# Output projection, second half: a third pair of K tiles by seven products

## The chip, the cores and the metric

One core of a Trainium2 chip runs the whole kernel in one launch. The metric is the device time in microseconds; lower is better. Engines are named as in the profile: PE (matrix products; PEld its weight loads), DVE and ACT (elementwise work), POOL, and SP, whose queue issues most DMA loads.

## The reference, cut to what matters

Two layers, 256 tokens, model width 2048. The part in question is the output projection of the mixer:

```
mix = concat([stick-breaking heads (8 x 128), differential heads (8 x 128)])   # (256, 2048)
m   = mix @ w_o                                                                # (256, 2048)
x   = x + rms_norm(m, post_mix_norm)
h   = rms_norm(x, pre_ffn_norm)
x   = x + rms_norm((silu(h @ w_gate) * (h @ w_up)) @ w_down, post_ffn_norm)
```

Everything is float32 in and out.

## The kernel before

**Tiles.** The 256 tokens are two token tiles of 128 (t = 0, 1). A weight matrix is cut into column blocks of 512 (c) and into pairs of K tiles of 128 (kp). One load of 512 KB brings a weight tile of one pair and one column block. Float32 products are made of three matmuls: each operand is split into a rounded part (`hi`, written by ACT) and the rest (`lo`, written by DVE), and PE does hi x hi, hi x lo, lo x hi. `feed` (L297) does this split for each weight in the order of the stream: ACT at L307, DVE at L317. `raw`, `hi` and `lo` are rings in `wpool` with 4, 6 and 6 places; a new tile waits until the readers of the tile six (four) places back are done.

**Eight and seven products.** Two K tiles, two token tiles and two column blocks make a 2 x 2 by 2 x 2 block product: eight products, 24 matmuls. For some pairs the kernel uses a form with seven products (Winograd's), 21 matmuls, in `seven_products`. It needs sums of the activations (`token_sums`, called by `pair_forms`: tiles f, s, sh, sl) and sums of the weights (`mixed_weights`, L263): from the two loaded tiles g and u ACT and DVE form in turn `hi`/`lo` of g, u + g (L285), `hi`/`lo` of that (L279, L281), differences (L290, L291), and the splits `T2h`/`T2l` and `Th`/`Tl`. Four extra PSUM banks (p1, p6, p7, q5) collect products over all seven-product pairs of a stage; `shared_part` (L1125 to L1129) folds them into `mg` after the last such pair, and L1179 adds a part of `mg` to the still open sums of token tile 1.

**Output projection.** Its first half does column blocks 0 and 1 over all eight pairs while the last attention heads are still being finished. The second half does blocks 2 and 3. `LATE_O` gives the order of pairs there, `LAST_O` the two pairs that come at the very end, done token tile by token tile so that the norm of tile 0 can begin while PE works on tile 1; `O_SEVEN` names the pairs with seven products. In this kernel the order is 4, 5, 0, 1, 6, 2 and then 3, 7, with seven products for 5 and 6. Their token sums are computed in the first half, after units 9 and 11 (L1157), in places of the ring `tok`; their weights are loaded into places of the attention's ring `v` (two), and `T2h`/`T2l` lie in `ah` and `al` (one each).

**The end of the stage.** From `feed(idx + 6)` on the order of ACT and DVE is the program's (`manual_schedule`). `evac_sum` takes the sums of token tile 0 out (L589 adds `mg`, L591 squares, L592 multiplies by the gain), `rescale` forms the norm and writes `x` (L627), PE transposes it (L485), ACT and DVE split it into `xF` (L488, L493), and the gate and up products of the next stage (L1250) start. Elsewhere a scheduler orders each engine's instructions by its own costs; each engine then runs its queue in that order.

Of the kernel before, what the change touches and what calls it, by code (L numbers as in the profile page):

```python
# [9 lines left out]
F32 = mybir.dt.float32  # L10
F32R = mybir.dt.float32r
# [6 lines left out]
P = 128  # L18
D = 2048
S = 256  # L20
# [5 lines left out]
CW = 512  # L26
# [5 lines left out]
URGENT = 50  # L32
TAIL = 3
KP_O = (4, 5, 6, 7, 0, 1, 2, 3)
LATE_O = (4, 5, 0, 1, 6, 2)
LAST_O = (3, 7)
O_SEVEN = (5, 6)
PAIRS = ((6, 8), (10, 7), (9, 0), (11, 2), (1, 3), (4, 5))
IN_SEVEN = (4, 5)
IN_ORDER = (0, 1, 4, 2, 5, 3, 6, 7)  # L40
# [40 lines left out]
def weight_order():  # L81
# [9 lines left out]
    for l in range(L):  # L91
# [7 lines left out]
        order_o = [(c, kp) for kp in KP_O for c in (0, 1)]  # L99
        order_o += [(c, kp) for kp in LATE_O for c in (2, 3)] + [(c, kp) for c in (2, 3) for kp in LAST_O]  # L100
        lay["order_o"] = order_o
# [66 lines left out]
def kernel(  # L168
# [35 lines left out]
    order, plan, sevens, plain, own = weight_order()  # L204
# [3 lines left out]
    for lay in plan:  # L208
        for c in range(1, FF // CW):
            for n in (1, 2):  # L210
                helped[lay["gate"][c, gate_order(c)[n]]] = n == 1
    newest_seven = [None]

    ready = {}
    raws, loads = [], []
# [2 lines left out]
    def fetch(upto):  # L218
        while len(raws) < min(upto, len(stream)):
            i = len(raws)  # L220
            for j in range(i, min(i + EARLY + 1, mix_raw[3])):
                if j in sevens and j not in sums:
                    summed(j)
            if i in sevens:
                raws.append(sums[i])
                continue
            if i + 1 in sevens:
                g = mix_raw[0].tile([P, 2, CW], F32, tag="G", bufs=mix_raw[1], name=f"G{i}")
                with not_ahead(i):
                    loads.append(nc.sync.dma_start(g, stream[i]))  # L230
                raws.append(g)
                continue
            if i in own or i + 1 in own:
                raw = mix_pool[0].tile([P, 2, CW], F32, tag="v", bufs=2, name=f"V{i}")
            elif i in plain or i + 1 in plain:
                raw = late_room([P, 2, CW], f"GU{i}")
            else:
                raw = wpool.tile([P, 2, CW], F32, tag="raw", bufs=4, name=f"raw{i}")
            mixing = bool({i, i + 1} & (own | plain))
            with not_ahead(i) if mixing else nullcontext():  # L240
                loads.append(nc.sync.dma_start(raw, stream[i]))
            raws.append(raw)
            if not mixing:
                usual.append((i, loads[-1]))
# [15 lines left out]
    mix_pool = [None]  # L260
    mix_raw = [None, 0, 0, 0]

    def mixed_weights(i):  # L263

        g, u = raws[i - 1], raws[i]
        hi = wpool.tile([P, 2, CW], F32R, tag="hi", bufs=6, name=f"hi{i}")
        lo = wpool.tile([P, 2, CW], F32R, tag="lo", bufs=6, name=f"lo{i}")
        if i in own:
            th = wpool.tile([P, 2, CW], F32R, tag="hi", bufs=6, name=f"Th{i}")
            tl = wpool.tile([P, 2, CW], F32R, tag="lo", bufs=6, name=f"Tl{i}")  # L270
            th2 = mix_pool[0].tile([P, 2 * (S + P)], F32R, tag="ah", bufs=1, name=f"T2h{i}")[:, 0:CW]
            tl2 = mix_pool[0].tile([P, 2 * (S + P)], F32R, tag="al", bufs=1, name=f"T2l{i}")[:, 0:CW]
        else:
            th = mix_pool[0].tile([P, 3, CW], F32R, tag="Th", bufs=1 if i in plain else 2, name=f"Th{i}")
            tl = mix_pool[0].tile([P, 3, CW], F32R, tag="Tl", bufs=1 if i in plain else 2, name=f"Tl{i}")
            th2, tl2 = th[:, 2, :], tl[:, 2, :]

        def split(h, l, w):
            nc.scalar.activation(h, w, AF.Copy)  # L279
            with in_row(i):  # L280
                newest_rest[i] = nc.vector.tensor_tensor(out=l, in0=w, in1=h.bitcast(F32), op=ALU.subtract)  # L281

        if i in plain or i in own:
            with after_rests():
                nc.vector.tensor_tensor(out=u[:, 0, :], in0=g[:, 0, :], in1=u[:, 0, :], op=ALU.add)  # L285
        split(hi, lo, u)
        t1, b22 = ((hi[:, k, :], lo[:, k, :]) for k in range(2))
        t3, t4 = ((th[:, k, :], tl[:, k, :]) for k in range(2))
        t2 = u[:, 1, :]
        nc.vector.tensor_tensor(out=t2, in0=t2, in1=u[:, 0, :], op=ALU.subtract)  # L290
        nc.vector.tensor_tensor(out=g, in0=g, in1=t2.unsqueeze(1).to_broadcast([P, 2, CW]), op=ALU.add)  # L291
        split(th2, tl2, t2)
        split(th[:, 0:2, :], tl[:, 0:2, :], g)
        t2 = th2, tl2
        return {"b22": b22, "t1": t1, "t2": t2, "t3": t3, "t4": t4}
# [645 lines left out]
    def pair_forms(pool, spool, bufs, tiles, kp, nm, **kw):  # L941
        f = pool.tile([P, 2, S], F32, tag="t2", name=f"f{nm}_{kp}")
        for kk in range(2):
            st = tiles[2 * kp + kk]
            nc.vector.tensor_tensor(out=f[:, kk, :], in0=st[:, 0, :].bitcast(F32), in1=st[:, 1, :].bitcast(F32), op=ALU.add)
        return token_sums(pool, spool, bufs, f[:, 0, 0:P], f[:, 1, 0:P], f[:, 0, P:S], f[:, 1, P:S], f"{nm}_{kp}", **kw)
# [138 lines left out]
        nc.tensor.matmul(a, sh, lo, start=False, stop=False, skip_group_check=open_sums[0])  # L1085
        return nc.tensor.matmul(a, sl, hi, start=False, stop=last, skip_group_check=open_sums[0])  # L1086

    def token_sums(pool, spool, bufs, a11, a12, a21, a22, nm, tags=("sh", "sl")):

        s = pool.tile([P, 4, P], F32, tag="t2", name=f"s{nm}")  # L1090
        nc.vector.tensor_tensor(out=s[:, 0, :], in0=a21, in1=a22, op=ALU.add)
        nc.vector.tensor_tensor(out=s[:, 1, :], in0=s[:, 0, :], in1=a11, op=ALU.subtract)
        nc.vector.tensor_tensor(out=s[:, 2, :], in0=a11, in1=a21, op=ALU.subtract)
        nc.vector.tensor_tensor(out=s[:, 3, :], in0=a12, in1=s[:, 1, :], op=ALU.subtract)
        if spool is None:
            both = late_room([P, 2, 4, P], f"ss{nm}", F32R)
            sh, sl = both[:, 0], both[:, 1]
        else:
            sh = spool.tile([P, 4, P], F32R, tag=tags[0], bufs=bufs, name=f"sh{nm}")
            sl = spool.tile([P, 4, P], F32R, tag=tags[1], bufs=bufs, name=f"sl{nm}")  # L1100
        nc.scalar.activation(sh, s, AF.Copy)
        nc.vector.tensor_tensor(out=sl, in0=s, in1=sh.bitcast(F32), op=ALU.subtract)
        return [(sh[:, j, :], sl[:, j, :]) for j in range(4)]
# [31 lines left out]
    for l in range(L):  # L1135

        pool = Rooms(tc, f"att{l}")
# [5 lines left out]
        mix, mixed = {}, set()  # L1143
# [6 lines left out]
        forms = {}  # L1150
        for n, (c, kp) in enumerate(plan[l]["order_o"][:16]):
            run_until(lambda: mixed >= {2 * kp, 2 * kp + 1})
            unit({t: accs[c, t] for t in range(NT)}, mix, plan[l]["o"][c, kp], kp, range(NT), kp == KP_O[0], kp == KP_O[-1])
            if kp == KP_O[-1]:
                for t in range(NT):
                    evac_chunk(pool, accs[c, t], mg, ssm, gpost, c, t, f"o{l}")
            if n in (9, 11):  # L1157
                kp = O_SEVEN[(n - 9) // 2]
                forms[kp] = pair_forms(pool, pool, 4, mix, kp, f"o{l}", tags=("tok", "tok"))
        got = four_banks(True, [f"o{l}_{c}_{t}" for t in range(NT) for c in (2, 3)])  # L1160
        accs = {(c, t): got[2 * t + c - 2] for c in (2, 3) for t in range(NT)}
        open_sums[0] = True
        for kp in LATE_O:
            i, j = (plan[l]["o"][c, kp] for c in (2, 3))
            if kp not in O_SEVEN:
                for c, i in ((2, i), (3, j)):
                    unit({t: accs[c, t] for t in range(NT)}, mix, i, kp, range(NT), kp == LATE_O[0], False)
                continue
# [12 lines left out]
        xT = x_tiles(f"xF{l}")  # L1181
        idx = plan[l]["o"][2, LAST_O[0]]
        last_o = [(c, kp) for c in (2, 3) for kp in LAST_O]
        with tc.manual_schedule(engines={mybir.EngineType.Activation, mybir.EngineType.DVE}):
            feed(idx + 6)
            for n, (c, kp) in enumerate(last_o):
                unit({0: accs[c, 0]}, mix, idx + n, kp, (0,), False, kp == LAST_O[-1], 0)
                if kp == LAST_O[-1]:
                    evac_sum(pool, accs[c, 0], mg, ssm, gpost, c, 0, f"o{l}")
# [16 lines left out]
        pool = tc.alloc_tile_pool(name=f"ffn{l}", bufs=5, reuse_waits="tile")  # L1206
        gu = tc.alloc_tile_pool(name=f"gu{l}", bufs=1, reuse_waits="tile")
# [5 lines left out]
        forms = {}  # L1213
# [45 lines left out]
        for c in range(FF // CW):  # L1259
# [9 lines left out]
            for n, kp in enumerate(order):  # L1269
# [13 lines left out]
                if kp == mine[-1]:  # L1283
                    w = [pool.tile([P, CW], F32, tag="t2", name=f"w{j}_{l}_{c}") for j in range(4)]
# [38 lines left out]
        for half in range(2):  # L1323
            split, forms = {}, {}
# [73 lines left out]
            for t in range(NT):  # L1398
# [4 lines left out]
                for c in cc:  # L1403
                    for kp in range(nkp - tail, nkp):
# [4 lines left out]
                        for kk in range(2):  # L1409
                            sh, sl = jh[:, kk, t * P : (t + 1) * P], jl[:, kk, t * P : (t + 1) * P]  # L1410
# [64 lines left out]
```

## Time and profile before

| | |
|---|---|
| time, median of 3 runs | 2182.53 us (2181.71 to 2182.81) |
| profiled execution, device time | 2183.48 us |
| its span, first to last instruction | 2181.7 us |
| busy PE / DVE / ACT / POOL | 2166.0 / 1920.7 / 1400.4 / 260.5 us |
| second half of the output projection, first layer | about 350.8 to 393 us |
| the same, second layer | about 1436.8 to 1479 us |
| granted clock of TensorE | 0.999 |

Times in the profile count from the first instruction of the span. A row of a timeline gives start, duration, engine, line, operation, output and inputs, count, and in brackets how long the engine was idle before it and what it waited for. A row of the chain gives start, length, engine and line. A row of the groups ends with the busy time of all, the mean in ns of one, and the idle time before them. A row of the waits gives the total, the number and the longest. A row of a windows view gives the length, then busy time and number of instructions of PE, PEld, DVE, ACT and POOL, the clock, the DMA share and GB/s. A matmul's duration overlaps the next one's, so its cost is read from the starts. All lines are those of the kernel before.

### The profile page before, as it was taken

The numbers are of one execution on the slowest core, as the hardware profiler recorded it, in microseconds if no ns is written. First come the engines' busy times: TensorE is split into PE (matmuls) and PEld (weight loads), VectorE is DVE, ScalarE is ACT, GpSimd is POOL, SyncE is SP. The second block draws the span as 40 slices with busy tenths as digits, with TensorE's granted clock in tenths as the row PEclk, the third lists the DMA queues.
The fourth block names the chain that finished last, engine by engine and source line by source line (L and its number), as shares of the span: only waits on it lengthen the run. The fifth ranks groups of instructions, "written<-read, shape, count | busy, mean of one in ns | idle before, by whom it ended". The sixth has DMA issues, their size and how long they took to land.

```text
span 2181.7 us, 28784 instructions
## 1 busy us (share of the span) xinstructions
PE 2166.0 (99%) x9944; PEld 1781.7 (82%) x9944; DVE 1920.7 (88%) x2657; ACT 1400.4 (64%) x2089; POOL 260.5 (12%) x243
## 2 busy tenths in 40 slices
PE   9999999999999999999999999999999999999998
PEld 7888888788888888888878888887888888888886
DVE  7888658899999999999878886589999999999997
ACT  7666665756666656666665666657666666576664
POOL 1100000031222221000010000000212222200000
PEclk9999999999999999999999999999999999999999
DMA  9544555488887767767465555555888877768683
GB/s 323 194 164 174 193 184 176 165 300 234 239 258 229 226 231 233 239 223 258 149 241 174 172 174 188 191 164 191 286 237 241 262 222 227 240 225 244 204 268 100
DMA packets 140851, 471.49 MB, mean 216 GB/s; under 512 B 16016, under 2 KB 17040, under 8 KB 140192
## 3 DMA queue, kind: packets, MB, share of 16 engines
q1 hardware_dynamic: 121952, 436.03, 57.7%
q0 software_dynamic: 18176, 33.07, 9.2%
q8 instruction: 78, 1.28, 0.2%
q14 instruction: 69, 0.57, 0.1%
q10 hardware_dynamic: 576, 0.54, 0.1%
HBM read 461.19 MB, written 8.39 MB: 215 GB/s over the span
## 4 chain that ended last, share of the span: by engine, by line
PE 94%; DVE 3%; ACT 2%; issue 1%; DMA 0%; SPq 0%; DVEq 0%; ACTq 0%
PE c L1250 19%; PE in L1084 7%; PE in L1086 7%; PE in L1085 7%; PE dn L1357 4%; PE dn L1356 4%; PE dn L1359 4%; PE p L1085 3%; PE c L1084 3%; PE p L1084 3%; PE p L1086 3%; PE c L1085 3%; PE c L1086 3%; PE o L569 2%; PE o L571 2%; PE o L570 2%
## 5 line engine op out<-in xcount | busy, mean ns | idle before, releaser
L317 DVE TENSOR_TENSOR lo<-raw,hi 128x1024 fp32r<-128x1024 f32 x468 | 561.9, 1220 | 103.3 <-ACT hi L307 102.3
L307 ACT ACTIVATE hi<-raw 128x1024 fp32r<-128x1024 f32 x490 | 501.5, 1053 | 102.3 <-DMA raw<-in_weights_in_turn_dram 41.8
L1250 PE MATMUL c<-hi,xF 128*128 128x512 f32 x1280 | 345.9, 391 | 1.5 <-DVE xF L493 1.5
L1250 PEld LDWEIGHTS c<-hi,xF 128*128 128x128 f32 x1280 | 238.3, 188 | 50.3 <-DVE xF L493 2.0
L258 POOL DMA_DIRECT2D T<-in_weights_in_turn_dram x126 | 111.2, 883 | 1373.8 <-DMA T<-in_weights_in_turn_dram 716.6
L1250 PE MATMUL c<-lo,xF 128*128 128x512 f32 x640 | 198.2, 390 | 2.5 <-DVE lo L317 2.5
L279 ACT ACTIVATE Th<-G 128x1024 fp32r<-128x1024 f32 x126 | 133.1, 1056 | 79.8 <-DVE G L291 78.6
L281 DVE TENSOR_TENSOR Tl<-G,Th 128x1024 fp32r<-128x1024 f32 x126 | 153.9, 1221 | 10.1 <-ACT Th L279 10.1
L1356 PE MATMUL dn<-hi,jh 128*128 128x512 f32 x416 | 162.0, 389 | 0.0
L1357 PE MATMUL dn<-lo,jh 128*128 128x512 f32 x416 | 161.8, 389 | 0.0
L307 ACT ACTIVATE hi<-G 128x1024 fp32r<-128x1024 f32 x126 | 132.9, 1055 | 44.6 <-DMA G<-in_weights_in_turn_dram 27.8
L281 DVE TENSOR_TENSOR lo<-T,hi 128x1024 fp32r<-128x1024 f32 x126 | 159.6, 1266 | 0.3 <-ACT hi L279 0.2
L279 ACT ACTIVATE Th<-T 128x512 fp32r<-128x512 f32 x126 | 79.7, 633 | 118.6 <-DVE T L290 113.3
L291 DVE TENSOR_TENSOR G<-G,T 128x1024 f32<-128x1024 f32 x126 | 153.5, 1218 | 1.8
L1250 PEld LDWEIGHTS c<-lo,xF 128*128 128x128 f32 x640 | 120.1, 188 | 28.1 <-DVE lo L317 3.0
L317 DVE TENSOR_TENSOR lo<-G,hi 128x1024 fp32r<-128x1024 f32 x108 | 131.6, 1219 | 12.3 <-ACT hi L307 12.2
L279 ACT ACTIVATE hi<-T 128x1024 fp32r<-128x1024 f32 x126 | 132.2, 1049 | 12.1 <-PE c L1086 10.6
L1084 PE MATMUL in<-hi,xT 128*128 128x512 f32 x328 | 131.0, 401 | 0.6 <-DVE xT L862 0.6
L1084 PE MATMUL in<-hi,xI 128*128 128x512 f32 x328 | 131.1, 401 | 0.0
L1085 PE MATMUL in<-lo,xI 128*128 128x512 f32 x328 | 128.0, 390 | 0.3 <-DVE lo L317 0.3
L1085 PE MATMUL in<-lo,xT 128*128 128x512 f32 x328 | 127.8, 391 | 0.4 <-DVE lo L891 0.4
L1359 PE MATMUL dn<-hi,jl 128*128 128x512 f32 x416 | 128.0, 389 | 0.0
(485 smaller groups left out, 4954.2 us busy)
## 6 DMA issues: line engine op xcount, KB each, us to landing
raw<-in_weights_in_turn_dram SPq DMA_DIRECT2D x490, 512.0 KB, 4.6
T<-in_weights_in_turn_dram SPq DMA_DIRECT2D x126, 512.0 KB, 5.3
G<-in_weights_in_turn_dram SPq DMA_DIRECT2D x126, 512.0 KB, 5.4
T<-in_weights_in_turn_dram POOLq DMA_DIRECT2D x126, 256.0 KB, 6.1
GU<-in_weights_in_turn_dram SPq DMA_DIRECT2D x32, 512.0 KB, 6.5
V<-in_weights_in_turn_dram SPq DMA_DIRECT2D x8, 512.0 KB, 3.7
away_ffn<-x SPq DMA_DIRECT2D x8, 512.0 KB, 8.2
xd<-away_ffn SPq DMA_DIRECT2D x8, 512.0 KB, 9.4
```

The costliest lines, as they stand in the source:

```text
L279: nc.scalar.activation(h, w, AF.Copy)
L281: newest_rest[i] = nc.vector.tensor_tensor(out=l, in0=w, in1=h.bitcast(F32), op=ALU.subtract)
L291: nc.vector.tensor_tensor(out=g, in0=g, in1=t2.unsqueeze(1).to_broadcast([P, 2, CW]), op=ALU.add)
L307: nc.scalar.activation(hi, raw, AF.Copy)
L317: rest = nc.vector.tensor_tensor(out=lo, in0=raw, in1=hi.bitcast(F32), op=ALU.subtract)
L1084: nc.tensor.matmul(a, sh, hi, start=first, stop=False, skip_group_check=open_sums[0])
L1085: nc.tensor.matmul(a, sh, lo, start=False, stop=False, skip_group_check=open_sums[0])
L1086: return nc.tensor.matmul(a, sl, hi, start=False, stop=last, skip_group_check=open_sums[0])
L1250: nc.tensor.matmul(a, stat[part], w[j][:, kk, :], start=first and kk + n == 0, stop=last and kk == 1 and n == 2)
L1356: nc.tensor.matmul(accs[c, t], sh, hi[:, kk, :], start=first, stop=False, skip_group_check=open_sums[0])
L1357: nc.tensor.matmul(accs[c, t], sh, lo[:, kk, :], start=False, stop=False, skip_group_check=open_sums[0])
L1359: nc.tensor.matmul(accs[c, t], sl, hi[:, kk, :], start=False, stop=last, skip_group_check=open_sums[0])
```

## The change

The second half's pairs now come in the order 4, 5, 1, 7, 6, 2 and then 0, 3, and pair 7 too is done with seven products, at the fourth place. Its token sums are formed after unit 11, those of pairs 5 and 6 two units earlier than before. The added pair's tiles take places of other rings: the sums sh and sl in the ring `a`, the two loaded weight tiles in `qk` (so they no longer take places of `raw`), `T2` in `w`; `Th` and `Tl` take places of `hi` and `lo`, as for the other two.

```diff
-LATE_O = (4, 5, 0, 1, 6, 2)
-LAST_O = (3, 7)
-O_SEVEN = (5, 6)
+LATE_O = (4, 5, 1, 7, 6, 2)
+LAST_O = (0, 3)
+O_SEVEN = (5, 7, 6)
+O_FORM_AT = {7: 5, 9: 6, 11: 7}
...
+    between = {lay["o"][3, O_SEVEN[1]] for lay in plan}
+    set_aside = []
...
-            if i in own or i + 1 in own:
+            if i in between or i + 1 in between:
+                raw = set_aside.pop(0)
+            elif i in own or i + 1 in own:
                 raw = mix_pool[0].tile([P, 2, CW], F32, tag="v", bufs=2, name=f"V{i}")
...
-            th2 = mix_pool[0].tile([P, 2 * (S + P)], F32R, tag="ah", bufs=1, name=f"T2h{i}")[:, 0:CW]
-            tl2 = mix_pool[0].tile([P, 2 * (S + P)], F32R, tag="al", bufs=1, name=f"T2l{i}")[:, 0:CW]
+            th2, tl2 = (
+                mix_pool[0].tile([P, 2 * (S + P)], F32R, tag="w" if i in between else t, bufs=3 if i in between else 1, name=f"T2{t}{i}")[:, 0:CW]
+                for t in ("ah", "al")
+            )
...
-            if n in (9, 11):
-                kp = O_SEVEN[(n - 9) // 2]
-                forms[kp] = pair_forms(pool, pool, 4, mix, kp, f"o{l}", tags=("tok", "tok"))
+            if n in O_FORM_AT:
+                kp = O_FORM_AT[n]
+                if kp == O_SEVEN[1]:
+                    forms[kp] = pair_forms(pool, pool, 2, mix, kp, f"o{l}", tags=("a", "a"), width=2 * (S + P))
+                else:
+                    forms[kp] = pair_forms(pool, pool, 4, mix, kp, f"o{l}", tags=("tok", "tok"))
+            if n == 11:
+                set_aside[:] = [pool.tile([P, 2, CW], F32, tag="qk", bufs=4, name=f"V{q}_o{l}") for q in "gu"]
```

`token_sums` gets a `width` for places that are wider than the sums; nothing else changes in it.

More of the change, by code (lines that the diff above doesn't have):

```diff
@@ L1086, in product, with token_sums @@
         return nc.tensor.matmul(a, sl, hi, start=False, stop=last, skip_group_check=open_sums[0])
-    def token_sums(pool, spool, bufs, a11, a12, a21, a22, nm, tags=("sh", "sl")):
+    def token_sums(pool, spool, bufs, a11, a12, a21, a22, nm, tags=("sh", "sl"), width=4 * P):
         s = pool.tile([P, 4, P], F32, tag="t2", name=f"s{nm}")
@@ L1098, in token_sums @@
         else:
-            sh = spool.tile([P, 4, P], F32R, tag=tags[0], bufs=bufs, name=f"sh{nm}")
-            sl = spool.tile([P, 4, P], F32R, tag=tags[1], bufs=bufs, name=f"sl{nm}")
+            sh, sl = (
+                spool.tile([P, width], F32R, tag=tag, bufs=bufs, name=f"{q}{nm}")[:, 0 : 4 * P].rearrange("p (j n) -> p j n", j=4)
+                for q, tag in zip(("sh", "sl"), tags)
+            )
         nc.scalar.activation(sh, s, AF.Copy)
```

## The prediction

> **What bounds the kernel now.** I read the page first, then TensorE's waits over the whole span, then the chain that ended last, then the timelines of PE and DVE through the output projection of the first layer.
>
> ```profile
> span 2181.7 us, 28784 instructions
> ...
> PE 2166.0 (99%) x9944; PEld 1781.7 (82%) x9944; DVE 1920.7 (88%) x2657; ACT 1400.4 (64%) x2089; POOL 260.5 (12%) x243
> ```
>
> PE is without work for 2181.7 - 2166.0 = 15.7 us. So a product taken out of PE's queue is worth its time only where nothing else is late next. Where PE waits:
>
> ```profile
> PE c L1250 <- DVE lo L317: 2.5, 2, 1.3
> ...
> PE c L1250 <- DVE xF L493: 1.5, 2, 0.7
> ```
>
> Both waits are two of a kind, one in each layer, and both sit at the seam behind the output projection, where the gate products (`c`, L1250) start. The chain shows what stands ahead of them:
>
> ```profile
> 384.38 1.07 ACT hi L307
> 385.48 1.23 DVE lo L317
> ...
> 392.23 0.76 DVE x L627
> ...
> 406.21 3.70 PE c L1250 x15
> ...
> 1470.35 1.07 ACT hi L307
> ...
> 1492.17 3.75 PE c L1250 x15
> ```
>
> From 384.38 to 406.21 the end of the kernel hangs on ACT and DVE: two gate weights are split, the first token tile's sums are taken out (L589), the norm is formed, `x` is written (L627), transposed, split into `xF`. The second layer repeats it: 1470.35 to 1492.17 is 21.82 us, 384.38 to 406.21 is 21.83 us. Whatever this chain's start loses, the kernel loses, twice; PE's products beside it are cover.
>
> **What is removed: three matmuls a layer.** A pair of eight products issues 24 matmuls, one of seven 21; the order of instructions of the changed program has six rows fewer on PE. What is one worth?
>
> ```profile
> L569 PE MATMUL o<-hi,mix_sb 128*128 128x512 f32 x128 | 50.2, 392 | 0.0
> ...
> L569 PEld LDWEIGHTS o<-hi,mix_sb 128*128 128x128 f32 x128 | 24.0, 188 | 5.0
> ```
>
> ```profile
> 361.00 0.39 PE L569 MATMUL o<-hi,mix_sb 128*128 128x512 f32 x1
> ...
> 376.64 0.39 PE L569 MATMUL o<-hi,mix_sb 128*128 128x512 f32 x1
> ...
> 381.41 0.40 PE L569 MATMUL o<-hi,mix_sb 128*128 128x512 f32 x1
> ...
> 384.18 0.39 PE L569 MATMUL o<-hi,mix_df 128*128 128x512 f32 x1
> ...
> 393.04 1.32 PE L485 MATMUL xT_ps<-ident,x 128*128 128x128 f32 x8
> ...
> 396.42 1.19 PE L1250 MATMUL c<-hi,xF 128*128 128x512 f32 x4 [0.74 <-DVE xF L493]
> ```
>
> Not 392 ns: from 361.00 to 376.64 pairs 0, 1 and 6 start 24 + 24 + 21 = 69 matmuls, 15.64 / 69 = 0.227 us from start to start. So 3 x 0.227 = 0.68 us a layer, 1.36 us in all, and by itself it ends at 2182.53 - 1.36 = 2181.2. The Trainium skill (Perfetto Trace Analysis, Identifying the Most-Contended Engine) calls matmul busy time a bad measure because matmuls are pipelined, and takes the LDWEIGHTS busy time in its place: by the 188 ns of the second row six matmuls would be 1.13 us. I keep the spacing.
>
> **What is added on DVE and ACT.** The next rows are DVE's timeline.
>
> ```profile
> 332.38 0.75 DVE L945 TENSOR_TENSOR fo<-mix_df 128x256 f32<-128x256 f32 x2
> 333.05 0.28 DVE L1093 TENSOR_TENSOR so<-fo 128x128 f32<-128x128 f32 x1
> ...
> 336.46 0.68 DVE L1102 TENSOR_TENSOR slo<-so,sho 128x512 fp32r<-128x512 f32 x1
> ...
> 357.58 2.59 DVE L317 TENSOR_TENSOR lo<-raw,hi 128x1024 fp32r<-128x1024 f32 x2 [1.07 <-ACT hi L307]
> 360.31 1.23 DVE L317 TENSOR_TENSOR lo<-V,hi 128x1024 fp32r<-128x1024 f32 x1
> ...
> 363.40 1.22 DVE L281 TENSOR_TENSOR lo<-V,hi 128x1024 fp32r<-128x1024 f32 x1 [1.26 <-ACT hi L279]
> ...
> 367.81 1.23 DVE L281 TENSOR_TENSOR Tl<-V,Th 128x1024 fp32r<-128x1024 f32 x1 [0.61 <-ACT Th L279]
> 368.96 1.22 DVE L317 TENSOR_TENSOR lo<-raw,hi 128x1024 fp32r<-128x1024 f32 x1
> ...
> 375.80 0.68 DVE L1126 TENSOR_TENSOR mg_o<-p_o,mg_o 128x512 f32<-128x512 f32 x1
> ...
> 379.27 0.68 DVE L1128 TENSOR_TENSOR mg_o<-q_o,mg_o 128x512 f32<-128x512 f32 x1
> 379.87 0.68 DVE L1129 TENSOR_TENSOR mg_o<-q_o,mg_o 128x512 f32<-128x512 f32 x1
> ...
> 384.10 1.23 DVE L317 TENSOR_TENSOR lo<-raw,hi 128x1024 fp32r<-128x1024 f32 x1 [2.35 <-ACT hi L307]
> 385.48 1.23 DVE L317 TENSOR_TENSOR lo<-raw,hi 128x1024 fp32r<-128x1024 f32 x1 [0.16 <-ACT hi L307]
> 386.62 0.68 DVE L589 TENSOR_TENSOR mg_o<-o,mg_o 128x512 f32<-128x512 f32 x1
> ```
>
> The token sums of the added pair (two additions of 0.75 together, four of 0.28, one split of 0.68: 2.6 us of DVE) are computed in the first half. That stretch has room:
>
> ```profile
> 318.00:351.00 33.00, 33.00 (x160) 27.57 (x159) 24.44 (x44) 18.57 (x38) 0.00 (x0) 1.00 0.46 158
> ```
>
> DVE is free for 33.00 - 24.44 = 8.6 us there, PE never waits, so I cost the sums at nothing; without that cover they would cost at most their 2.6 us.
>
> The weight chain of a seven pair is another matter. Pair 6 holds DVE from 360.31 to 368.96, 8.65 us, ACT's answers included, while its 21 matmuls take 4.76 us. In the changed order of DVE pair 1's two splits move to the place of pair 0's, so pair 7's chain starts at 357.58, on the same freed `hi` place, and pair 6's behind it:
>
> 357.58 + 8.65 + 8.65 = 374.88. At this point DVE was at 368.96 before, 5.9 us earlier, though PE now needs the tiles 0.68 us sooner.
>
> Behind that the changed order has, one after another: four splits (pair 2, then pairs 0 and 3 for column block 2), L1126, L1127, the split of pair 0 for block 3, L1128, L1129, the first of the two L1179. Splits follow at 1.14 (385.48 to 386.62), additions at 0.60 (379.27 to 379.87), a dependent one at its 0.68 and 0.03. So 374.88 + 4 x 1.14 + 0.71 + 0.60 + 1.14 + 2 x 0.60 + 0.68 = 383.77 us for the end of that L1179. PE's second token tile may add to its open sums only after it.
>
> **What moves on PE.** Pair 2's products for the second token tile wait for L1179 in both kernels, but the changed order puts them later. Before, 21 matmuls lie between the start of pair 2 and them (376.64 to 381.41); after, 31: pair 2's first tile (12), pair 0 (6), pair 3 (6), pair 0 of block 3 (6), one of pair 3. PE alone would be there at 376.64 - 0.68 + 31 x 0.227 = 383.0; with L1179 it is 383.8. Twelve matmuls end at 386.5, where they ended at 384.18 before: 2.35 us later.
>
> **Who waits for that.** Two `hi` places become free with these products. ACT's gate splits wait for them (384.38 in the chain), DVE's `lo` behind ACT (384.10 with 2.35 us idle, 385.48), and L589, whose bank is long full, stands behind both `lo` in DVE's queue: 386.62. That is the head of the chain above. All 21.8 us of it follow 2.35 us later; PE runs out of projection at about 393 as before and stands until `x` arrives, which it used to get just in time (393.04). The 0.74 us wait before 396.42 grows by it.
>
> Sum: +2.35 us a layer, with the 0.68 us already in it; +4.7 in two. The profiled execution (2183.48 us, 1.8 us of it outside the span) lies 0.95 above the median, and both shift alike: 2182.53 + 4.7 = 2187.2 us.
>
> **The unknown term: a load.** Pair 7 leaves the `raw` ring of four, so the weight of pair 0 for block 3 gets the place of pair 2's first, free at 374.88 + 1.23 = 376.1 (before: 370.2, after the split of 368.96). How long does such a load take?
>
> ```profile
> DMA to landing us min/median/max: 3.3/4.3/5.0
> ```
>
> That is the raw loads issued from 366 to 380. I take 3.3, the row's least, since nothing else is being fetched then; it lands at 379.4, ACT's 1.06 us end before DVE comes to it (380.75). At 5.0 DVE stands 1.4 us at this split and the layer loses 3.75. At the other end, if DVE keeps up everywhere, PE's order alone costs (31 - 21 - 3) x 0.227 = 1.6 a layer. So +3.2 to +7.5 us, 2185.7 to 2190.0. Below that only if the chain has slack which I do not see: the first L627 of 392.23 is 0.76 long, the transposes start at 393.04.
>
> The other edits I cost at nothing. The two `qk` places of the added weights were last read for the scores; their loads stand in SP's queue right behind pair 2's, ahead of pair 6's. `w` and `a` places are past their last attention reader. The gate stage's first `G` load now waits for DVE, behind whose later work the raw loads of its queue wait anyway.
>
> **Rivals.**
> 1. *The gain arrives* (other side): -1.36 us, 2181.2. It needs DVE's lag gone before PE reaches pair 2's second tile: from 383.77 back to 380.7 at least, and the `hi` places free in time. For it: PE is busy for 99% of the span. Against: PE's order is fixed, and 31 matmuls stand where 21 stood. 0.05. The Trainium skill (Perfetto Trace Analysis, Identifying Performance Opportunities) says to work on the most contended engine first; by that rule this rival would be the outcome.
> 2. *The seam absorbs it*: the waits of 0.74 and 1.25 us behind the projection (2.5 + 1.5 in two layers by the waits' rows) shrink as the chain slips. Then 2.35 - 1.99 = 0.4 a layer, 2183.3. It decides if what is late there is not a successor of L589. Against: 392.23 to 406.21 is one unbroken chain. 0.08.
> 3. *The late load holds DVE*: 3.75 a layer, 2190.0. It decides above a landing of 3.5 us. For it: the median of 4.3; against: the empty queue. 0.17.
>
> My case, around 2.35 a layer, gets 0.70.
>
> **How the numbers follow.** 0.2% (4.4 us) is about what a measurement of this kernel can tell from no change, and my forecast of 4.7 lies just above. From my case I give 0.42 to slower and 0.28 to within; rival 3 is slower; rivals 1 and 2 are within it, save 0.02 for a gain I have no mechanism for. Faster 0.02, same 0.39, slower 0.59. The range, 2184.5 to 2189.8, leaves out rivals 1 and 2 and the far end of rival 3 (0.07): 0.20.
>
> **What would show it.** In the changed profile's DVE timeline L589 should stand about 2.35 us later than 386.62, with a wait of PE for DVE at pair 2's second tile, and PE's wait for DVE's `xF` at the first `c` should be near 3 us instead of 0.74. Pair 6's last `lo` (`Tl`) should end near 375, at most 0.2 us after PE asks. If L589 comes at 386 or earlier, my DVE sum is wrong; if it is late and `c` still starts at 396.4, the chain has slack that I did not see; if the `lo` of pair 0 for block 3 waits for ACT's `hi` for over a microsecond, rival 3 is at work.

## The result, and the profile after

The changed kernel takes 2190.08 us (median of 5 runs, 2187.72 to 2192.13) against 2182.53 (2181.51 to 2183.36): 1.0035 times, 95% interval 1.0024 to 1.0047, or +7.55 us. Forecast was 2187.2 us, at most 2189.8: the sign was right, the size too small. Line numbers moved: L1179 is now L1193, L589 L596, L592 L599, L627 L634, L485 L492, L1250 L1264, L317 L324, L281 L288, L230 L233, L257 and L258 L262 and L263.

DVE's timeline in the second half of the projection, first layer, after the change:

```profile
357.20 1.22 DVE L324 TENSOR_TENSOR lo<-Vg_o,hi 128x1024 fp32r<-128x1024 f32 x1 [1.07 <-ACT hi L314]
...
365.86 1.22 DVE L324 TENSOR_TENSOR lo<-V,hi 128x1024 fp32r<-128x1024 f32 x1
...
373.36 1.23 DVE L288 TENSOR_TENSOR Tl<-V,Th 128x1024 fp32r<-128x1024 f32 x1 [0.61 <-ACT Th L286]
374.51 4.62 DVE L324 TENSOR_TENSOR lo<-raw,hi 128x1024 fp32r<-128x1024 f32 x4
...
380.44 1.22 DVE L324 TENSOR_TENSOR lo<-raw,hi 128x1024 fp32r<-128x1024 f32 x1
...
382.77 1.29 DVE L1193 TENSOR_TENSOR o<-o,mg_o 128x512 f32<-128x512 f32 x2
...
386.31 2.60 DVE L324 TENSOR_TENSOR lo<-raw,hi 128x1024 fp32r<-128x1024 f32 x2 [1.12 <-ACT hi L314]
388.82 0.68 DVE L596 TENSOR_TENSOR mg_o<-o,mg_o 128x512 f32<-128x512 f32 x1
...
394.43 2.74 DVE L634 SCALAR_TENSOR_TENSOR x<-mg_o,tot_o,x 128x512 f32<-128x512 f32 x4
```

The two weight chains stand back to back: pair 7 from 357.20, pair 6 from 365.86 (8.66 us for the first), the last `Tl` done at 374.59. `L596` starts at 388.82 where L589 started at 386.62, and `x` at 394.43 instead of 392.23: 2.2 us later, all the way to the first long run of `c`. The stage itself, from its first product `o` on, began 0.39 us earlier in this execution (298.27 against 298.66), so measured from its own start the delay is 2.6 us. The chain of waits:

```profile
382.86 0.62 DVE o L1193
383.52 0.50 PE o L576
386.58 1.08 ACT hi L314
387.68 1.23 DVE lo L324
...
394.43 0.76 DVE x L634
395.24 0.67 PE xT_ps L492 x4
...
408.41 3.70 PE c L1264 x15
412.55 1.40 PE c L1264 x6
414.38 1.17 PE c L1264 x5
415.56 11.29 DMA T<-in_weights_in_turn_dram
427.01 1.06 ACT hi L286
```

408.41 was 406.21. On PE, pair 2's products for the second token tile come after 31 matmuls, as forecast, and wait for DVE's sums only a little:

```profile
383.52 0.50 PE L576 MATMUL o<-hi,mix_sb 128*128 128x512 f32 x1 [0.15 <-DVE o L1193]
```

But the chain then goes on through something that it did not hold before: an accumulating `T` load that takes 11.29 us. Who is waited for, from the views of the waits (PE over the whole span, then ACT from 400 to 500 us):

```profile
PE xT_ps L492 <- DVE x L634: 4.2, 2, 2.1
PE p L1092 <- DVE Tl L288: 3.6, 3, 1.7
PE c L1264 <- DVE lo L324: 2.3, 2, 1.3
...
ACT hi L286 <- DMA T<-in_weights_in_turn_dram: 2.9, 1, 2.9
```

PE stands 2.1 us a layer for `x` (the forecast's mechanism) and, which no part of the forecast has, for `Tl` of the gate stage's first seven-product pairs. Behind that `Tl` is the load. SP's queue and POOL's, before (the first three rows) and after (the next three), and DVE's last `x` after:

```profile
406.60 0.90 SPq L257 DMA_DIRECT2D T<-in_weights_in_turn_dram  x2
407.54 0.93 SPq L230 DMA_DIRECT2D G<-in_weights_in_turn_dram  x2
411.57 0.89 POOL L258 DMA_DIRECT2D T<-in_weights_in_turn_dram  x1 [261.72 <-DMA T<-in_weights_in_turn_dram]
```

```profile
408.80 0.90 SPq L262 DMA_DIRECT2D T<-in_weights_in_turn_dram  x2
412.81 0.80 SPq L233 DMA_DIRECT2D G<-in_weights_in_turn_dram  x2
413.55 0.89 POOL L263 DMA_DIRECT2D T<-in_weights_in_turn_dram  x1 [264.09 <-DMA T<-in_weights_in_turn_dram]
```

```profile
412.03 0.75 DVE L634 SCALAR_TENSOR_TENSOR x<-mg_o,tot_o,x 128x512 f32<-128x512 f32 x1
```

The `T` loads moved by the chain's 2.2 us, the two `G` loads by 5.3. My reading is that the first `G` tile overlaps the last `qk` place (no view shows addresses; the times and e1 and e2 below bear it out). In the kernel before the late sum tile of token tile 0 lay there; the two added weight tiles, which take their `qk` places first, shift the ring so that token tile 1's tile lies there, and its last reader is the last `x`, done at 412.78; `G` is issued at 412.81. In the second layer the two stand 0.03 us apart as well (1503.44 and 1503.47), while in the kernel before `G` directly follows `T` on SP's queue. So `G` starts beside the accumulating loads instead of four microseconds ahead of them. The accumulating loads in the DMA views, 404 to 430 us, before and after (count, KB, median us to landing):

```profile
T<-in_weights_in_turn_dram POOLq DMA_DIRECT2D x2, 256.0 KB, 6.8
```

```profile
T<-in_weights_in_turn_dram POOLq DMA_DIRECT2D x2, 256.0 KB, 10.5
```

To see what each part costs, I cut each profiled execution by events on PE: the first product `o` of the projection, the first `c`, and the first transposes of the gate stage's results (starts as the timeline of PE has them). Us for each stretch:

| kernel | projection, layer 1 | layer 2 | first gate chunks, layer 1 | layer 2 | sum against before |
|---|---|---|---|---|---|
| before | 97.8 | 97.7 | 86.1 | 86.3 | |
| after | 100.4 | 100.3 | 88.7 | 87.8 | +9.3 |
| a2 | 100.3 | 100.3 | 87.2 | 89.2 | +9.2 |
| e1 | 100.4 | 100.4 | 86.1 | 87.2 | +6.1 |
| e2 | 97.7 | 97.7 | 87.8 | 87.6 | +3.0 |
| e3 | 97.6 | 97.5 | 86.2 | 86.3 | -0.3 |
| e5 | 99.1 | 99.1 | 86.2 | 86.4 | +2.9 |
| e6 | 98.8 | 98.9 | 86.2 | 86.5 | +2.5 |
| e11 | 99.4 | 99.5 | 87.1 | 85.9 | +4.0 |
| e15 | 100.3 | 100.3 | 88.5 | 88.8 | +10.1 |

So the changed kernel's profiled execution (2191.98 us, 1.9 above the median) loses 2.6 us in each of the two projections and 2.5 + 1.5 us behind them. All other stretches together are 0.7 us shorter than before (span 2190.3 against 2181.7: 8.6).

### The profile page after: what moved, and what is told of

The parts are those of the page before. It is cut to its first block, busy times and chain, and to the rows that moved or that the text cites. A ratio compares the mean times of both kernels' runs of the same rounds, so it can differ in the third digit from the quotient of the medians.

```text
span 2190.3 us, 28799 instructions
## 1 busy us (share of the span) xinstructions
PE 2167.4 (99%) x9938; PEld 1782.0 (81%) x9938; DVE 1936.9 (88%) x2681; ACT 1404.1 (64%) x2095; POOL 261.3 (12%) x243
## 4 chain that ended last, share of the span: by engine, by line
PE 87%; DVE 7%; ACT 2%; issue 2%; DMA 2%; DVEq 0%; ACTq 0%; SPq 0%; POOLq 0%
PE c L1264 17%; PE in L1091 7%; PE in L1093 7%; PE in L1092 7%; PE dn L1373 4%; PE dn L1370 4%; PE dn L1371 4%; PE p L1092 3%; PE p L1093 3%; PE c L1091 3%; PE c L1092 3%; PE c L1093 3%; PE p L1091 3%; DVE lo L324 2%; PE o L576 2%
## 5 line engine op out<-in xcount | busy, mean ns | idle before, releaser
L324 DVE TENSOR_TENSOR lo<-raw,hi 128x1024 fp32r<-128x1024 f32 x464 | 557.4, 1222 | 91.2 <-ACT hi L314 90.1
L314 ACT ACTIVATE hi<-raw 128x1024 fp32r<-128x1024 f32 x486 | 495.7, 1052 | 90.8 <-DMA raw<-in_weights_in_turn_dram 46.6
L1264 PE MATMUL c<-hi,xF 128*128 128x512 f32 x1280 | 346.3, 392 | 0.7 <-DVE xF L500 0.7
L1264 PEld LDWEIGHTS c<-hi,xF 128*128 128x128 f32 x1280 | 238.6, 188 | 49.7 <-DVE xF L500 1.3
L263 POOL DMA_DIRECT2D T<-in_weights_in_turn_dram x126 | 110.8, 880 | 1378.6 <-DMA T<-in_weights_in_turn_dram 769.1
L1264 PE MATMUL c<-lo,xF 128*128 128x512 f32 x640 | 198.2, 390 | 2.3 <-DVE lo L324 2.3
L288 DVE TENSOR_TENSOR Tl<-G,Th 128x1024 fp32r<-128x1024 f32 x126 | 154.0, 1223 | 9.8 <-ACT Th L286 9.8
L288 DVE TENSOR_TENSOR lo<-T,hi 128x1024 fp32r<-128x1024 f32 x126 | 159.5, 1266 | 2.5 <-ACT hi L286 2.3
L1264 PEld LDWEIGHTS c<-lo,xF 128*128 128x128 f32 x640 | 120.1, 188 | 27.9 <-DVE lo L324 2.8
L324 DVE TENSOR_TENSOR lo<-G,hi 128x1024 fp32r<-128x1024 f32 x108 | 131.9, 1221 | 11.0 <-ACT hi L314 11.0
```

Source lines behind the costliest of these rows:

```text
L314: nc.scalar.activation(hi, raw, AF.Copy)
L324: rest = nc.vector.tensor_tensor(out=lo, in0=raw, in1=hi.bitcast(F32), op=ALU.subtract)
L1264: nc.tensor.matmul(a, stat[part], w[j][:, kk, :], start=first and kk + n == 0, stop=last and kk == 1 and n == 2)
```

## The experiments

Theory A: two costs, the projection's chain of DVE and the `G` loads on a place that comes free late. Theory B: one cost, the chain and what follows from it. Each kernel was timed against the kernel before on its own chip.

**e1 and e2: the places alone.** The same line in the changed kernel (e1) and in the kernel before (e2), ahead of `shared_part`, a memset of one element a partition:

```diff
+                nc.vector.memset(mg[1, 1][:, 0, 0:1], 0.0)
```

Who writes first gets the next place of the ring, so in both the two late sum tiles change places: in e1 `G` is free of the late tile, in e2 it comes under it.

> The changed kernel with one memset of one element of the second token tile's sum, ahead of the shared part: it is the first to ask for a qk place, so the two late sum tiles change places, and the one that is read last no longer lies under the gate stage's first G tile. Theory A (two costs: the projection's chain, 2.2 us a layer, and the G load that waits for DVE's last x and then runs beside the accumulating T loads): the chain stays, the collision goes: 2182.5 + 2 x 2.2 = 2187.0 us, the G loads are issued about 410 instead of 412.8, no T load lands later than about 7 us. Theory B (all of the 7.5 us is the projection's chain and what follows from it): 2190 us as the changed kernel.

> The kernel before (two pairs of seven) with the same memset: here it puts the sum tile that is read last under the gate stage's first G tile, nothing else moves. Theory A: the G loads wait for the last x of the projection, at about 410.6 instead of 407.5, and run beside the accumulating T loads of 411.6 and 412.9: the 3.1 us that the changed kernel has beyond its chain, 2185.6 us (2184 to 2187). Theory B: G is needed later than T, 2182.5 us.

Measured: e1 2187.82 us against 2182.16, +5.66 (ratio 1.0015 to 1.0035); e2 2184.78, +2.62 (1.0001 to 1.0019). In e1 (first row) `G` directly follows `T` again; in e2's projection nothing moved, but `G` (second row) starts only after the last `x`, done at 410.07:

```profile
409.71 0.93 SPq L233 DMA_DIRECT2D G<-in_weights_in_turn_dram  x2
```

```profile
410.09 0.81 SPq L230 DMA_DIRECT2D G<-in_weights_in_turn_dram  x2
```

In e2, PE and ACT show the changed kernel's waits (PE over the span; ACT in the second layer, 1490 to 1590 us):

```profile
PE p L1085 <- DVE Tl L281: 2.9, 3, 1.5
...
ACT hi L279 <- DMA T<-in_weights_in_turn_dram: 3.0, 1, 3.0
```

In e1 the projection's wait stays and the one for `Tl` all but goes:

```profile
PE xT_ps L492 <- DVE x L634: 4.2, 2, 2.1
...
PE p L1092 <- DVE Tl L288: 0.2, 1, 0.2
```

Theory A holds: without any third pair, the place alone costs 2.6 us (0.2 to 4.1 by the interval), and without the place the third pair alone costs 5.7 (3.3 to 7.6); together 8.3, where the changed kernel has 7.55. Of e1's cost, 0.9 us lie in the second layer's first gate chunks, which neither part of the theory explains; their cause stays open.

**a2: the changed kernel again**, beside e6, e11 and e13.

> The changed kernel itself, beside the other three of this call, to compare on one chip. Theory A (projection's chain 4.4 to 4.8 us in two layers, G load beside the accumulating T loads 3 to 4 us): 2190 us, 2 to 3 us above the same kernel with the old places of the sum tiles (2187.8). Theory B (no second cost): 2188 us.

2190.28 us against 2181.82, +8.46 (1.0022 to 1.0049): 2.8 us above e1, each against its own chip's kernel before; the two intervals overlap, so this difference alone would not settle it. The first accumulating load of the second layer took 11.34 us here, and ACT waited 5.0 us for it.

**e3: DVE's chains shortened.** The late sum tiles on their old places (here they reuse the two added weight tiles, without e1's memset), and the addition `u+g` of the late pairs' weights on POOL:

```diff
-        if i in plain or i in own:
+        if i in own:
+            nc.gpsimd.tensor_tensor(out=u[:, 0, :], in0=g[:, 0, :], in1=u[:, 0, :], op=ALU.add)
+        elif i in plain:
...
```

> The changed kernel with the late sum tiles on the places they had before, and the addition u+g of the seven pairs' weights on POOL instead of DVE. Theory A: DVE's two chains in a row lose the 0.61 us addition and most of the 1.26 us wait for ACT behind it, up to 3.7 us for both; the first sum for token tile 1 ends near 380 instead of 383.5, pair 2's products for that tile come after 17 matmuls more instead of 31, at 379.8, and the gate's hi places are free by 382.5, ahead of 384.2: the delay is gone, 2181 to 2183 us. If POOL takes long for the addition or slows DVE, up to 2187. A rival in which the late head of the chain does not come from DVE's chains: 2187 us.

2182.32 us against 2182.16 (0.9993 to 1.0011), 5.5 us below e1. POOL takes 1.52 and 1.30 us for what is 0.69 on DVE, but off the path. DVE's timeline of e3:

```profile
365.12 1.22 DVE L326 TENSOR_TENSOR lo<-V,hi 128x1024 fp32r<-128x1024 f32 x1
366.26 1.22 DVE L288 TENSOR_TENSOR lo<-V,hi 128x1024 fp32r<-128x1024 f32 x1
...
380.08 1.29 DVE L1198 TENSOR_TENSOR o<-o,Vu_o 128x512 f32<-128x512 f32 x2
...
386.14 0.68 DVE L598 TENSOR_TENSOR Vg_o<-o,Vg_o 128x512 f32<-128x512 f32 x1
...
391.75 1.41 DVE L636 SCALAR_TENSOR_TENSOR x<-mg_o,tot_o,x 128x512 f32<-128x512 f32 x2
```

The two `lo` follow each other at 1.14 us where DVE stood 1.26 us for ACT; the sums of token tile 1 come 2.7 us earlier, token tile 0's at 386.14 instead of 388.82. The 5.2 us of the two projections are gone (table). But not DVE alone changed: with the shorter chains the scheduler also put pair 2's products for the second token tile earlier on PE, after 17 matmuls instead of 31, and there PE now waits 1.14 us for DVE:

```profile
380.83 0.50 PE L578 MATMUL o<-hi,mix_sb 128*128 128x512 f32 x1 [1.14 <-DVE o L1198]
```

So e3 shows that the delay goes with DVE's chains and the order of PE that follows from them; it does not part the two.

**e7: the same addition on POOL in the kernel before.**

> The kernel before (two pairs of seven) with u+g of their late pairs on POOL: if the 5.5 us between e1 and e3 come from DVE's two chains in a row, this edit brings next to nothing here, where PE never waits for DVE at these products: 2182 us. If POOL's addition is a gain in itself: 2179 us or less.

2180.67 us against 2180.62 (0.9990 to 1.0009): nothing. e3's 5.5 us are no gain of POOL in itself.

**e5: the chains apart.** e1 with another order:

```diff
-LATE_O = (4, 5, 1, 7, 6, 2)
+LATE_O = (4, 5, 7, 1, 6, 2)
```

> The changed kernel with e1's memset and pair 7 one place earlier (order 4, 5, 7, 1, 6, 2), so that a pair of eight stands between the chains of pairs 7 and 6. Pair 2's products for token tile 1 come after 27 matmuls instead of 31 (21 in the kernel before). Theory A: 4 x 0.227 = 0.9 us a layer less than with the chains in a row, 2187.0 - 1.8 = 2185.2 us. If DVE's sum is what counts and not the order, no change: 2187.0 us.

2184.71 us, +2.55 (1.0003 to 1.0021), 3.1 below e1. The wait for `x` falls to 1.2 us a layer (2.4 in two), and the projections are 1.3 to 1.4 us a layer longer than before instead of 2.6. So half of the chain's cost was the place of pair 7 in the order: pair 2's second token tile comes after 27 matmuls instead of 31 there, and its sums from DVE 1.1 us earlier.

**e11 and e12: token tile 0's sums ahead of the gate's splits.** e11 is e1, e12 the kernel before, each with

```diff
...
-            feed(idx + 6)
+            feed(idx + 4)
...
             rescale(mg, ssm, 0, f"o{l}")
+            feed(idx + 6)
```

> e1 with the two gate weights' splits (ACT hi, DVE lo) moved behind the first token tile's x in the written order of ACT and DVE. Theory A (the first token tile's sums are only late because they stand behind these two lo in DVE's queue, and those behind hi places that PE frees late): the second sum of token tile 0 starts when its bank is full, at 387.7 instead of 391.0, x at about 390.5 instead of 394.4, the transposes follow the last products at 392.9 without a wait instead of 395.2: 2.3 us a layer less than e1, 2187.0 - 4.6 = 2182.4 to 2183.2 us. Rival (the first token tile's sums wait for their banks, or the gate's splits become the late ones): 2187 us or more, with a wait of c for lo.

> The kernel before with the two gate weights' splits behind the first token tile's x, as in e11. x comes earlier, but PE has products until 393.0, so nothing can be gained at the transposes; DVE's two lo (2.4 us) then stand ahead of its xF, and the first c waits for them: 1 to 1.5 us a layer later, 2184 to 2185 us. This is the part of e11's expected 4.6 us that did not come. If the splits cost nothing there: 2182 us.

e11: 2185.26 us, +3.44 (1.0006 to 1.0024); e12: 2184.71, +4.09 (1.0010 to 1.0027). In e11 the head of the chain does what the theory says:

```profile
385.46 0.69 DVE L596 TENSOR_TENSOR mg_o<-o,mg_o 128x512 f32<-128x512 f32 x1
...
388.07 0.69 DVE L596 TENSOR_TENSOR mg_o<-o,mg_o 128x512 f32<-128x512 f32 x1 [0.44 <-PE o L578]
...
391.60 2.74 DVE L634 SCALAR_TENSOR_TENSOR x<-mg_o,tot_o,x 128x512 f32<-128x512 f32 x4
394.26 3.49 DVE L324 TENSOR_TENSOR lo<-raw,hi 128x1024 fp32r<-128x1024 f32 x3
```

`x` comes 2.8 us earlier than in e1, and the second sum ahead of it now waits for PE's bank, so the head really stood behind the two `lo`. But only 2.2 of the expected 4.6 us came: three `lo` instead of one now stand ahead of DVE's `xF`, and PE waits there, in e11 and e12 alike:

```profile
PE c L1266 <- DVE xF L500: 5.3, 3, 2.3
```

e11's expectation priced the move and not what it moved into; e12's, written later, had this and was met.

**e6 and e13: the steps together.** e6 is e5 with e3's addition on POOL, e13 is e6 with e11's order.

> Pair 7 one place earlier (as e5) and u+g of the seven pairs on POOL (as e3), old places of the sum tiles. Pair 2's products for token tile 1 come after 21 matmuls, as in the kernel before. Theory A: PE no longer waits for DVE at these products (1.1 us a layer in e3), the 0.68 us of three matmuls reach the chain: x and the first c 0.7 to 1.1 us earlier than in the kernel before, 2181.0 us. Rival: POOL's additions or DVE's later work hold it at e3's 2182.3.

> e6 with the gate splits behind x as in e11. Theory A: PE is the limit of the projection's end, 0.7 us a layer less than in the kernel before: 2181.0 us. If the gate's splits are then late for the first c: up to 2184 us.

Both missed what was expected: e6 2183.68 us, +1.86 (0.9999 to 1.0017, so not clear of no change); e13 2187.66, +5.84 (1.0018 to 1.0039). In e6 the chain of waits shows a late weight:

```profile
373.07 4.48 DMA raw<-in_weights_in_turn_dram
377.65 1.07 ACT hi L316
378.74 1.23 DVE lo L326
...
381.83 0.50 PE o L578
```

DVE is faster, so it asks for the weights for block 3 sooner than the loads can come: it stands 0.54 us at pair 0's and 0.46 us at pair 3's, the one in these rows. That is the prediction's third rival, in a kernel other than the one it was written for. PE waits 1.5 us a layer for the sums behind it. e13 adds the wait for `xF` to it.

**e15: `G` still later, but behind the accumulating loads.** The changed kernel; the first two `G` loads of each gate stage go from SP's to POOL's queue, behind the two accumulating `T` loads (`added` is the list of these):

```diff
...
+                behind = i in (138, 140, 530, 532)
-                with not_ahead(i):
-                    loads.append(nc.sync.dma_start(g, stream[i]))
+                with tc.issue_after(added[-1].ins) if behind else not_ahead(i):
+                    loads.append((nc.gpsimd if behind else nc.sync).dma_start(g, stream[i]))
...
```

> The changed kernel with the first two G loads of each gate stage moved from SP's queue to POOL's, behind the two accumulating T loads: G comes some 3.6 us later still (416.4 instead of 412.8), but no longer ahead of the accumulating loads on the DMA engines. Theory A1 (the late G costs because it delays the accumulating loads beside it): these land in under 8 us again, and the second cost goes: 2187 to 2188 us. Theory A2 (G itself is what comes too late): the cost grows, 2192 us or more, with waits for G.

2191.34 us against 2180.62, +10.7 (1.0035 to 1.0061). The time lies in neither of the two expected ranges. The accumulating loads land in 5.4 us, sooner than in the kernel before, and ACT never waits for `T`:

```profile
G<-in_weights_in_turn_dram POOLq DMA_DIRECT2D x2, 512.0 KB, 6.4
T<-in_weights_in_turn_dram POOLq DMA_DIRECT2D x2, 256.0 KB, 5.4
```

So the long landing in the changed kernel does come from `G` beside it. The time did not come back, though: `G` now lands near 422 to 423, and the first gate chunks are 88.5 and 88.8 us long, about as in the changed kernel or longer. ACT also takes the token sums ahead of `G` there and stands 3.6 us for them, and `G` is on another queue, so I can't say how much of that is `G` itself. Shown is that a late `G` costs; whether it would without harming `T` stays open.

## Why the prediction was wrong in size

Point by point, by its own steps:

- **Three matmuls less, 0.68 us a layer.** Not to be seen alone: e3's projections are 0.2 us shorter than before, with 1.1 us of waiting for DVE inside, and the whole kernel is equal within 0.1%, which neither shows nor excludes 1.36 us.
- **Token sums at nothing.** Right: pair 7's chain, which stands where pair 0's splits stood, starts 58.9 us after the stage's first product, as those did.
- **Two chains back to back, 374.88; first L1179 done at 383.77.** Measured 374.59 and 383.48, or 374.98 and 383.87 with the 0.39 us by which the stage began earlier. Right within 0.1 us.
- **PE's order, `hi` places, the head of the chain.** Forecast +2.35 us a layer, 1.6 of it PE's order and the rest the wait for L1179; 2.6 in both layers of the profiled execution. The 31 matmuls are there. The waits for DVE ahead of pair 2's second tile add 0.9 us by the starts on PE: 0.3 at pair 6's `Tl`, 0.2 at pair 0's `lo` for block 3, 0.4 at L1193. So the mechanism is right and the term 0.5 us too small in two layers. e3 and e5 shorten the delay through DVE's chains and PE's order together, e11 through DVE's queue.
- **Where the wait shows.** I put it at `xF` ahead of the first `c` (0.74 growing to 3). It stands one step earlier, at the transposes, for `x` (2.1 a layer); in the first layer `c` for `xF` stayed at 0.74. The prediction had itself said that PE runs out of products at about 393, so this should have followed.
- **The late load.** I took 3.3 us and DVE just in time. Issued at 375.75, it let ACT start at 379.13, 3.4 us later, after 1.53 us of ACT waiting; its `hi` was done at 380.19, and DVE came to it at 380.44 and did not wait. Rival 3 did not decide, but by 0.25 us only: in e6 DVE is there before the load and waits 0.54 us.
- **Rival 2, the seam absorbs it.** No: the long run of `c` moved by the whole 2.2 us.
- **Rival 1, the gain.** Against: three matmuls fewer on the engine that is busy 99% of the span, and the kernel is slower. The rule that I set beside it, from the Trainium skill (Perfetto Trace Analysis, Identifying Performance Opportunities), names the engine to work on; the waits name what the work frees, and here it was DVE and a buffer place.
- **The step that failed:** "The gate stage's first `G` load now waits for DVE, behind whose later work the raw loads of its queue wait anyway." I saw the new wait in the order of instructions and costed it at nothing, by asking only what stands behind it in SP's queue. I did not ask until when it waits (the last `x`, 412.8, three microseconds after SP has issued the `T` loads), nor what the load then runs beside: the two accumulating loads on POOL's queue, which ACT waits for next. It costs 2.6 us in e2, 2.8 between e1 and a2, 4.0 in the profiled execution. The Trainium skill (DMA: Bandwidth & Descriptors, Rules for kernel authors) says that loads issued from different engines run on the same 16 DMA engines and interleave; the landing of 10.5 us beside `G`, and of 5.4 us ahead of it in e15, agrees.

With that term the sum is 4.7 + 2.6 to 2.8 = 7.3 to 7.5 us; 7.55 was measured. That this is so near is in part luck: the intervals of the runs are some microseconds wide, and the profiled execution has 5.2 + 4.0. The range missed by 0.3 us; with a cost for this wait at its upper end it would have held the result.

No version beats the kernel before: e3 and e7 are equal to it within 0.1%.

## What to carry to other kernels

A tile that takes a place of another ring shifts everything that the ring holds later. Follow each later holder to whoever next uses that memory: when is its last reader done, and what does the load that waits for it run beside? A wait that is "behind other work anyway" is free only if the time at which it ends was read off, too. And a saving on the busiest engine pays only if what feeds it has as much room: here the saved matmuls cost a second chain of 8.66 us on DVE, and the lever was to shorten or part those chains (5.5 and 3.1 us, with the order of PE that followed), not to drop products.

## What the runs showed of the hardware

Over both layers, the slower of the two accumulating loads of 256 KB landed in 5.6 to 7.7 us when the two 512 KB loads of `G` were issued behind it (e15) or four microseconds ahead of it (before, e1), and in 9.4 to 11.6 us when the first of these was issued 0.3 to 1.0 us ahead of it (after, a2, e2). `G` itself took 5.5 to 8.9 us in either case. Not only accumulating loads suffer: the plain `raw` load that SP issues 1.2 us behind `G` in these three kernels took 8.9 to 9.8 us, where the slowest `raw` load of the other three in that stretch took 3.8 to 7.6.

The run-to-run spread of the changed kernel, 4.4 us over 5 runs against 1.9 of the kernel before, may be that collision: ACT's wait for `T` was 2.9 us in the first layer of one profiled execution, and 0.7 and 5.0 in the two layers of another. That link was not tested.
